# Sums of squares on VectorE only, the row factor one quarter later in the feed-forward, and the rotation tables made later

## The chip, the cores and the metric

The kernel runs on one core of a Trainium2 chip. Its time is the device time of one launch in microseconds (us). A time is the median of several runs; beside it stands one execution that was taken with the hardware profiler, from which all rows come. TensorE is called PE in the rows, its weight load PEld, VectorE DVE, ScalarE ACT, GpSimd POOL, and SyncE SP.

## The reference

One sequence of 512 tokens of width 1024 in float32 goes through a block of two layers and then a second block. Cut to what matters:

```
x = x + 0.5 * swiglu(rmsnorm(x, g), w_gate, w_up, w_down)   # first feed-forward of a layer
x = x + mixed(rmsnorm(x, g)) @ w_out                        # pooling and dilated attention with rotated q and k
x = x + 0.5 * swiglu(rmsnorm(x, g), ...)                    # second feed-forward of the layer
...                                                         # the second layer, a final rmsnorm
x = x + second_mix(rmsnorm(x, g)); x = x + swiglu(rmsnorm(x, g), ...); out = rmsnorm(x, g)

def rmsnorm(x, g):  return x * rsqrt(mean(x * x, axis=-1) + 1e-6) * g
def rope_tables(positions):  ang = positions * inv_freq;  return cos(ang), sin(ang)
```

So there are five feed-forwards and three mixes, each with a norm ahead of it, and a norm at the end.

## The kernel before, in words

x lies transposed in eight tiles `x[c]` of 128 x 512 (width on partitions, tokens along a row). All large products are made in three passes of a two-part float32: an operand is split into a high part (`yh`, `wh`, on ACT) and a low part (`yl` at L456, `wl` at L371, on DVE), and PE makes high x high, low x high and high x low (L407 to L409 and L627 to L629).

**The norm.** The products are made of the raw x times the gain. The factor per token, 1/sqrt(mean square), comes in afterwards. `square` (L458) adds the squares of the eight tiles into `ss`: the first is written by ACT (L461), each other is squared into `sq` by ACT (L467), or by DVE (L465) for four tiles at the start, and added at L468, by GpSimd (`eng=G`) or by VectorE (`V`, the last two tiles, or every fourth). `row_factor` (L483) sums `ss` over the partitions by matmuls with ones (`tst`, L487) and takes the inverse root on DVE in some dozen small steps (L489, L476 to L481, the result is `rf`). `spread` (L501) turns the factor by PE into a row for each partition (`tbc`, L498) that ACT copies to `rbc` (L505). The evacuations of the first products multiply by `rbc` (`cc`, L568).

**The feed-forward** (`ffn`, L540) goes through eleven pairs of 256 columns in four phases. The first pair is plain: the quarters T11, T12, T21 and T22 of 24 matmuls of 128 x 512 each. Every other pair is made of seven products (W11, S1, S2, W12, S3, S4, W22) of 24 matmuls of 128 x 256; S1, S2 and the like take sums of quarters of x as an operand (`r`, L437 to L440, split into `rh`, L442, and `rl`, L443) and sums of weights (`wt`). W11 of the second pair writes a bank (`x1`) that one of the plain pair's results lay in, so it follows that result's evacuation. Each turn of the loop gives out one product; `row_factor` is called after turn 0 (T11) and `spread` after turn 1.

**The start** (L1559 on) loads x, splits and squares it, makes the rotation tables (`rope_tables`, L704, some 28 small DVE instructions and two ACT sines), and goes into the first feed-forward.

The order on each engine isn't that of the code line by line: a scheduler orders the instructions of each engine at build time by its own estimate, and the engines then keep to that order. What an edit moves is read from the order of each engine.

The places of the program, in time: the start (first feed-forward of layer 0); from mix 0 to the second feed-forward; from there to the first feed-forward of layer 1; from mix 1 to the second feed-forward of layer 1; mix 2; from mix 2 to the last feed-forward; the end.

Of the kernel before, what the change touches and what calls it, by code (L numbers as in the profile page):

```python
# [28 lines left out]
D = 1024  # L29
KC = D // P  # L30
# [13 lines left out]
G_FFN1, G_MIX, G_FFN2, G_FIN, G_MIX2, G_FFN3, G_FIN2, G_AB, G_PROD = 0, 2, 4, 6, 7, 8, 9, 10, 11  # L44
# [62 lines left out]
D_ORDER = (0, 4, 1, 5, 2, 6, 3, 7)  # L107
# [115 lines left out]
def tile_blocks(tc, A, out):  # L223
    nc = tc.nc
    V, ACT, G, PE = nc.vector, nc.scalar, nc.gpsimd, nc.tensor

    with (
# [14 lines left out]
        def tbank(name="tp"):  # L242
            return pst.tile([P, S], F32, name=name, tag="tp")
# [3 lines left out]
        x = [keep.tile([P, S], F32, name=f"x{c}") for c in range(KC)]  # L247
# [11 lines left out]
        def gain(i, c):  # L259
            return gains[:, i * KC + c : i * KC + c + 1]  # L260
# [150 lines left out]
        def cut(hl, *ix):  # L411
            return hl[0][ix], hl[1][ix]
# [3 lines left out]
        sums = {}  # L416
# [9 lines left out]
            return pair[c]  # L426

        def square_x(c):
            square(x[c], c == 0, V if c >= KC - 2 else G)

        def sums_of(c, g):

            b1, b2 = (state["ffn"].tile([P, 2, HALF], F32, name="b", tag="snap", bufs=3) for _ in range(2))
            r = state["ffn"].tile([P, 4, HALF], F32, name="r", tag="wt", bufs=2)
            ACT.activation(b1, x[c], AF.Copy, scale=gain(g, c))
            ACT.activation(b2, x[c + 4], AF.Copy, scale=gain(g, c + 4))
            V.tensor_sub(r[:, 0], b1[:, 0], b1[:, 1])  # L437
            V.tensor_sub(r[:, 2], b2[:, 1], b1[:, 1])
            V.scalar_tensor_tensor(r[:, 1], b2[:, 1], -1.0, r[:, 0], op0=ALU.mult, op1=ALU.subtract)
            V.scalar_tensor_tensor(r[:, 3], r[:, 1], -1.0, b2[:, 0], op0=ALU.mult, op1=ALU.subtract)  # L440
            h, l = rest[c] = [state["ffn"].tile([P, 4, HALF], F32R, name=f"r{e}{c}", tag=f"r{e}{c}", bufs=1) for e in "hl"]
            ACT.activation(h, r, AF.Copy)  # L442
            V.tensor_sub(l, r, h.bitcast(F32))  # L443
# [11 lines left out]
            ACT.activation(h, src, AF.Copy, scale=g)  # L455
            V.scalar_tensor_tensor(l, src, g, h.bitcast(F32), op0=ALU.mult, op1=ALU.subtract)  # L456

        def square(src, first, eng=G, on_vector=False):  # L458
            if first:
                sums["s"] = small.tile([P, S], F32, name="ss", tag="ss", bufs=1)  # L460
                ACT.activation(sums["s"], src, AF.Square)  # L461
            else:
                sq = small.tile([P, S], F32, name="sq", tag="sq", bufs=2)
                if on_vector:
                    V.tensor_mul(sq, src, src)  # L465
                else:
                    ACT.activation(sq, src, AF.Square)  # L467
                eng.tensor_add(sums["s"], sums["s"], sq)  # L468

        def rsqrt(r, v):  # L470

            n = r.shape[1]
            it = small.tile([P, 8], I32, name="rsi", tag="rsi")
            t = small.tile([P, 8], F32, name="rst", tag="rst")
            it, t = it[:, :n], t[:, :n]
            V.tensor_scalar(it, v.bitcast(I32), 1, None, op0=ALU.logical_shift_right)  # L476
            V.tensor_scalar(r.bitcast(I32), it, -1, 0x5F3759DF, op0=ALU.mult, op1=ALU.add)
            for _ in range(3):
                V.tensor_mul(t, r, r)
                V.scalar_tensor_tensor(t, t, -0.5, v, op0=ALU.mult, op1=ALU.mult)  # L480
                V.scalar_tensor_tensor(r, t, 1.5, r, op0=ALU.add, op1=ALU.mult)  # L481

        def row_factor(s, n, name):  # L483

            o = tbank("tst")
            for i in range(TC):
                PE.matmul(o[:, i : i + 1], s[:, i * P : (i + 1) * P], ones, start=True, stop=True)  # L487
            v = small.tile([P, TC], F32, name="rv", tag="rv")
            V.tensor_scalar(v, o[:, :TC], 1.0 / n, EPS, op0=ALU.mult, op1=ALU.add)  # L489
            r = small.tile([P, TC], F32, name=name, tag="rfac", bufs=6)  # L490
            rsqrt(r, v)
            return r

        def spread_out(r):

            o = tbank("tbc")
            for i in range(TC):
                PE.transpose(o[:, i * P : (i + 1) * P], r[:, i : i + 1].to_broadcast([P, P]), ident)  # L498
            return o

        def spread(r, b=None):  # L501
            o = spread_out(r)
            if b is None:
                b = small.tile([P, S], F32, name="rbc", tag="rbc", bufs=1)
            ACT.copy(b, o)  # L505
            return b
# [30 lines left out]
                t, j = [p.rearrange("p a b -> p (a b)") for p in rest[c]], ("S1", "S2", "S3", "W22").index(name)  # L537
            return cut(t, slice(None), slice(j * HALF, (j + 1) * HALF))

        def ffn(coef, nxt, gain_of=None):  # L540
            pool = state["ffn"]
            a, got, cc, snap = {}, {}, {}, {}
            later = []
# [11 lines left out]
            def flat(t, half):  # L555
                return t[:, half].rearrange("p a b -> p (a b)")
# [37 lines left out]
            def evac(t, o):  # L594
                if len(t) == 2:
                    d = t[1]
                    V.scalar_tensor_tensor(x[d], o, coef, x[d], op0=ALU.mult, op1=ALU.add)  # L597
                    if t[0] == len(PHASES) - 1:
                        nxt(d)
                    return  # L600
                _, p, n = t
                if n == "W12":
                    V.tensor_add(flat(chunk(2 * p), 0), o[n], snap["W11"])
                elif n == "S3":
                    V.scalar_tensor_tensor(flat(chunk(2 * p + 1), 1), o[n], -1.0, snap["S1"], op0=ALU.mult, op1=ALU.subtract)
                elif n == "S4":
                    V.tensor_add(flat(chunk(2 * p), 1), o[n], snap["S2"])
                    finish(2 * p)
                elif n == "W22":
                    finish(2 * p + 1)  # L610
                elif n in ("T12", "T22"):
                    finish(n == "T22", o)
# [29 lines left out]
            for i, t in enumerate(ffn_plan()):  # L642
                w = take()
                if len(t) == 2:
                    ks = [f for p in PHASES[t[0]] for f in (2 * p, 2 * p + 1)]
                    while any(f not in a for f in ks):
                        rest_of()
                    od = tbank("dn")
                    for k, f in enumerate(ks):
                        mm3(od, cut(w, slice(None), slice(k * P, (k + 1) * P)), a[f], k == 0, k == len(ks) - 1)  # L650
                    now = t, od
                elif t[2] in PLAIN:
                    if i % 2 == 0:
                        o = [xbank(j, "mm") for j in range(2)]
                    plain(o, w, i // 2, i % 2)
                    now = t, o
                else:
                    n = t[2]
                    if n == "W11":
                        o = {}  # L660
                        o["W11"] = o["S2"] = o["S3"] = o["W22"] = xbank(0, "x1")
                    elif n == "S1":
                        o["S1"] = o["S4"] = xbank(1, "x3")
                    elif n == "W12":
                        o["W12"] = xbank(2, "x2")
                    product(o[n], w, n, n in ("W11", "S1", "W12"))
                    now = t, dict(o)
                if before:
                    evac_act(*before)
                highs(state["next"] + SPLIT)  # L670
                if before:
                    evac(*before)
                rest_of()
                lows(state["next"] + SPLIT)
                before = now
                if i == 0:
                    r = row_factor(sums["s"], D, "rf")
                if i == 1:
                    got["rb"] = spread(r)
                if i < 4 and gain_of is not None:  # L680
                    sums_of(i, gain_of)
            evac(*before)


# [861 lines left out]
            return f  # L1546

        def square_d(d):
            square(x[d], d == 0, V if d % 4 == 3 else G)

        def next_mix(g):
            def f(d):
                split(d, g)
                square_d(d)

            return f
# [6 lines left out]
        with layers():  # L1563
            for c in range(KC):
                split(c, G_FFN1)
                if c == 0:
                    ahead(1)
            ahead(2)
            for c in range(KC):
                square(x[c], c == 0, V if c >= KC - 2 else G, c % 2 == 1)  # L1570
            rope_tables()
            ffn(0.5, next_mix(G_MIX), G_FFN1)
        mix(0, G_FFN2)
        with layers(G_FFN2):
            ffn(0.5, next_ffn(G_FFN1 + 1), G_FFN2)
# [7 lines left out]
        rb = spread_out(row_factor(sums["s"], D, "rf"))  # L1583
# [22 lines left out]
```

## Time and profile before

| what | value |
|---|---|
| median of 3 runs | 2533.16 us (2532.66 to 2533.94) |
| profiled execution, its own time | 2529.62 us |
| its span (first to last instruction) | 2527.8 us |
| PE busy | 2462.2 us, 97% of the span |
| DVE busy | 1964.1 us, 78% |
| ACT busy | 1315.2 us, 52% |
| POOL busy | 343.9 us, 14% |

PE is the engine to look at: what isn't its work is a wait, a start or an end. A busy share hides where the waits are, and a PE that is busy at half its clock counts as busy too; so the rows further down are read by place. The profiled execution took 1.8 us more than its span, and 3.5 us less than the median.

### The profile page before, as it was taken

The numbers are of one execution on the slowest core, as the hardware profiler recorded it, in microseconds if no ns is written. First come the engines' busy times: TensorE is split into PE (matmuls) and PEld (weight loads), VectorE is DVE, ScalarE is ACT, GpSimd is POOL, SyncE is SP. The second block draws the span as 40 slices with busy tenths as digits, with TensorE's granted clock in tenths as the row PEclk, the third lists the DMA queues.
The fourth block names the chain that finished last, engine by engine and source line by source line (L and its number), as shares of the span: only waits on it lengthen the run. The fifth ranks groups of instructions, "written<-read, shape, count | busy, mean of one in ns | idle before, by whom it ended". The sixth has DMA issues, their size and how long they took to land.

```text
span 2527.8 us, 39773 instructions
## 1 busy us (share of the span) xinstructions
PE 2462.2 (97%) x15714; PEld 2217.4 (88%) x15714; DVE 1964.1 (78%) x2895; ACT 1315.2 (52%) x2065; POOL 343.9 (14%) x498
## 2 busy tenths in 40 slices
PE   7999999999999999999999999999999999999997
PEld 6999988887999988999988888999988887799996
DVE  8887764788887778877755889887767887988775
ACT  5444443676544455444444676444455775654442
POOL 1000014432000000000014431000013553100001
PEclk8999999999999999999999999999999999999999
DMA  4333232213233332333232113333233311323322
GB/s 160 109 100 104 74 100 88 57 40 105 88 117 100 103 107 80 102 109 103 80 93 86 43 42 113 111 101 105 73 101 95 98 42 41 118 92 105 105 65 77
DMA packets 73338, 229.72 MB, mean 91 GB/s; under 512 B 9536, under 2 KB 9920, under 8 KB 73152
## 3 DMA queue, kind: packets, MB, share of 16 engines
q1 hardware_dynamic: 73152, 227.19, 29.1%
q8 instruction: 123, 2.02, 0.3%
q14 instruction: 63, 0.52, 0.1%
HBM read 225.06 MB, written 2.10 MB: 90 GB/s over the span
## 4 chain that ended last, share of the span: by engine, by line
PE 84%; DVE 10%; ACT 3%; issue 2%; POOL 1%; DMA 1%; SPq 0%; DVEq 0%; ACTq 0%; POOLq 0%
PE x L629 13%; PE x L628 13%; PE x L627 13%; PE dn L407 8%; PE dn L408 8%; PE dn L409 8%; PE mm L407 5%; PE mm L408 5%; PE mm L409 4%; DVE wl L371 2%; PE ov L1028 2%; PE tp L1010 1%; PE mm L767 1%; PE mm L768 1%; DVE yl L456 1%
## 5 line engine op out<-in xcount | busy, mean ns | idle before, releaser
L627 PE MATMUL x<-rh,wh 128*128 128x256 f32 x1600 | 454.6, 284 | 4.0 <-ACT rh L442 3.8
L628 PE MATMUL x<-rl,wh 128*128 128x256 f32 x1600 | 454.6, 284 | 2.3 <-DVE rl L443 2.3
L629 PE MATMUL x<-rh,wl 128*128 128x256 f32 x1600 | 454.6, 284 | 0.0
L363 ACT ACTIVATE wh<-wd 128x768 fp32r<-128x768 f32 (+2 forms) x265 | 237.5, 896 | 348.6 <-PE x L628 173.6
L407 PE MATMUL dn<-ah,wh 128*128 128x512 f32 x880 | 344.0, 391 | 0.1
L408 PE MATMUL dn<-al,wh 128*128 128x512 f32 x880 | 343.8, 391 | 0.0
L409 PE MATMUL dn<-ah,wl 128*128 128x512 f32 x880 | 342.3, 389 | 0.0
L627 PE MATMUL x<-yh,wh 128*128 128x256 f32 x1200 | 339.7, 283 | 0.3 <-ACT wh L363 0.3
L628 PE MATMUL x<-yl,wh 128*128 128x256 f32 x1200 | 339.7, 283 | 0.0
L629 PE MATMUL x<-yh,wl 128*128 128x256 f32 x1200 | 339.6, 283 | 0.0
L627 PEld LDWEIGHTS x<-rh,wh 128*128 128x128 f32 x1600 | 308.5, 193 | 7.2 <-ACT rh L442 4.2
L363 ACT ACTIVATE wh<-wr 128x1024 fp32r<-128x1024 f32 (+1 forms) x178 | 187.5, 1054 | 241.6 <-PE x L628 88.9
L628 PEld LDWEIGHTS x<-rl,wh 128*128 128x128 f32 x1600 | 308.7, 193 | 5.0 <-DVE rl L443 2.7
L468 POOL TENSOR_TENSOR ss<-ss,sq 128x512 f32<-128x512 f32 x48 | 72.5, 1510 | 1762.3 <-ACT sq L467 1739.4
L629 PEld LDWEIGHTS x<-rh,wl 128*128 128x128 f32 x1600 | 308.4, 193 | 0.4 <-DVE wl L371 0.3
L371 DVE TENSOR_TENSOR wl<-wd,wh 128x768 fp32r<-128x768 f32 (+2 forms) x265 | 272.7, 1029 | 45.9 <-ACT wh L363 43.2
L371 DVE TENSOR_TENSOR wl<-wr,wh 128x1024 fp32r<-128x1024 f32 (+1 forms) x166 | 209.2, 1262 | 71.9 <-ACT wh L363 71.2
L627 PEld LDWEIGHTS x<-yh,wh 128*128 128x128 f32 x1200 | 230.2, 192 | 3.2 <-ACT wh L363 0.9
L628 PEld LDWEIGHTS x<-yl,wh 128*128 128x128 f32 x1200 | 230.3, 192 | 2.3
L629 PEld LDWEIGHTS x<-yh,wl 128*128 128x128 f32 x1200 | 230.1, 192 | 0.0
L597 DVE SCALAR_TENSOR_TENSOR x<-dn,x 128x512 f32<-128x512 f32 x160 | 110.0, 688 | 116.0 <-PE dn L409 116.0
L409 PEld LDWEIGHTS dn<-ah,wl 128*128 128x128 f32 x880 | 165.3, 188 | 35.3
(331 smaller groups left out, 5433.2 us busy)
## 6 DMA issues: line engine op xcount, KB each, us to landing
wr<-in_w SPq DMA_DIRECT2D x175, 512.0 KB, 3.6
wd<-in_w SPq DMA_DIRECT2D x120, 384.0 KB, 3.1
wq<-in_w SPq DMA_DIRECT2D x78, 512.0 KB, 3.6
wd<-in_w SPq DMA_DIRECT2D x55, 512.0 KB, 3.7
wd<-in_w SPq DMA_DIRECT2D x40, 256.0 KB, 3.1
x<-in_xT SPq DMA_DIRECT2D x8, 256.0 KB, 6.3
out<-x SPq DMA_DIRECT2D x8, 256.0 KB, 2.0
bias<-in_consts SPq DMA_DIRECT2D x2, 448.0 KB, 4.1
```

The costliest lines, as they stand in the source:

```text
L363: ACT.activation(h[:, :n], src[:, :n], AF.Copy)
L371: state["low"] = eng.tensor_sub(l[:, :n], src[:, :n], h[:, :n].bitcast(F32)).ins
L407: PE.matmul(o, w[0], xx[0], start=start, stop=False)
L408: PE.matmul(o, w[0], xx[1], start=False, stop=False)
L409: PE.matmul(o, w[1], xx[0], start=False, stop=stop)
L456: V.scalar_tensor_tensor(l, src, g, h.bitcast(F32), op0=ALU.mult, op1=ALU.subtract)
L468: eng.tensor_add(sums["s"], sums["s"], sq)
L597: V.scalar_tensor_tensor(x[d], o, coef, x[d], op0=ALU.mult, op1=ALU.add)
L627: PE.matmul(oo, wh, xh, start=start and j == 0 and c == 0, stop=False, skip_group_check=True)
L628: PE.matmul(oo, wh, xl, start=False, stop=False, skip_group_check=True)
L629: PE.matmul(oo, wl, xh, start=False, stop=c == 3, skip_group_check=True)
L1028: PE.matmul(o, w, part, start=(j == 0 and n == 0), stop=(j == TC - 1 and n == 1))
```

## The change

Three edits:

1. Every addition into `ss` (L468) is made on VectorE; the 48 that GpSimd made move there, 18 were there already. At the start the four squares that DVE made (L465) are made by ACT.
2. In `ffn`, `row_factor` is called in turn 1 and `spread` in turn 2, each ahead of that turn's evacuations, in place of the ends of turns 0 and 1.
3. `rope_tables` isn't called ahead of the first feed-forward, but handed to it as `aside`, and called behind the first down product of the third phase.

```
         def square_x(c):
-            square(x[c], c == 0, V if c >= KC - 2 else G)
+            square(x[c], c == 0)
...
-        def square(src, first, eng=G, on_vector=False):
+        def square(src, first, on_vector=False):
...
-                eng.tensor_add(sums["s"], sums["s"], sq)
+                V.tensor_add(sums["s"], sums["s"], sq)
...
-        def ffn(coef, nxt, gain_of=None):
+        def ffn(coef, nxt, gain_of=None, aside=None):
...
+                if i == 1:
+                    r = row_factor(sums["s"], D, "rf")
+                if i == 2:
+                    got["rb"] = spread(r)
                 if before:
                     evac_act(*before)
...
-                if i == 0:
-                    r = row_factor(sums["s"], D, "rf")
-                if i == 1:
-                    got["rb"] = spread(r)
                 if i < 4 and gain_of is not None:
                     sums_of(i, gain_of)
+                if aside and t == (2, D_ORDER[0]):
+                    aside()
...
-            square(x[d], d == 0, V if d % 4 == 3 else G)
+            square(x[d], d == 0)
...
-                square(x[c], c == 0, V if c >= KC - 2 else G, c % 2 == 1)
-            rope_tables()
-            ffn(0.5, next_mix(G_MIX), G_FFN1)
+                square(x[c], c == 0)
+            ffn(0.5, next_mix(G_MIX), G_FFN1, rope_tables)
```

The order on PE at the start, before: `tst` stands among the last products of the second 24-matmul quarter, `tbc` ten matmuls ahead of the first L627, which is W11 of the second pair.

```order
L407 MATMUL mm<-yh_138,wh 128x512
L408 MATMUL mm<-yl_139,wh 128x512
L409 MATMUL mm<-yh_138,wl 128x512
L487 MATMUL tst<-ones,ss 128x1 x4
L407 MATMUL mm<-yh_142,wh 128x512
...
L498 MATMUL tbc<-consts,rf 128x128 x4
L409 MATMUL mm<-yh_130,wl 128x512
...
L409 MATMUL mm<-yh_142,wl 128x512
L627 MATMUL x_429<-yh_108,wh 128x256
```

The same place on PE with the change.

```order
L407 MATMUL mm<-yh_122,wh 128x512
L408 MATMUL mm<-yl_123,wh 128x512
L487 MATMUL tst<-ones,ss 128x1 x4
L409 MATMUL mm<-yh_122,wl 128x512
...
L407 MATMUL mm<-yh_142,wh 128x512
L408 MATMUL mm<-yl_143,wh 128x512
L409 MATMUL mm<-yh_142,wl 128x512
L498 MATMUL tbc<-consts,rf 128x128 x4
L627 MATMUL x_389<-yh_108,wh 128x256
```

`tst` moved by 11 matmuls, into the third quarter, and `tbc` to the place directly ahead of W11. In the other feed-forwards the same two moved as well. From mix 0 to its feed-forward `tst` comes 24 matmuls later, and of the 29 matmuls between `tbc` and W11 10 are left; from the second feed-forward to the first of layer 1 24 of 38 are left, and from mix 2 to the last feed-forward 12 of 23.

The order on DVE from mix 0 to its feed-forward, before: `x_78` to `x_81` are the last four tiles of x, `yl_6239` to `yl_6251` their low parts, and five additions into `ss` are on POOL.

```order
L443 TENSOR_TENSOR rl_6319<-r,rh_6318 128x1024
L468 TENSOR_TENSOR ss<-ss,sq 128x512
L972 TENSOR_TENSOR x_81<-mm,x_81 128x512
L456 SCALAR_TENSOR_TENSOR yl_6239<-x_78,gains,yh_6238 128x512
L456 SCALAR_TENSOR_TENSOR yl_6243<-x_79,gains,yh_6242 128x512
L468 TENSOR_TENSOR ss<-ss,sq 128x512
L456 SCALAR_TENSOR_TENSOR yl_6247<-x_80,gains,yh_6246 128x512
L456 SCALAR_TENSOR_TENSOR yl_6251<-x_81,gains,yh_6250 128x512
L371 TENSOR_TENSOR wl<-wr,wh 128x1024
```

The same place on DVE with the change (its lines have moved by two, L974 is L972 of before).

```order
L438 TENSOR_TENSOR r<-b 128x256
L468 TENSOR_TENSOR ss<-ss,sq 128x512
L974 TENSOR_TENSOR x_80<-mm,x_80 128x512
L439 SCALAR_TENSOR_TENSOR r<-b,r 128x256
L456 SCALAR_TENSOR_TENSOR yl_6239<-x_78,gains,yh_6238 128x512
L456 SCALAR_TENSOR_TENSOR yl_6243<-x_79,gains,yh_6242 128x512
L468 TENSOR_TENSOR ss<-ss,sq 128x512
L974 TENSOR_TENSOR x_81<-mm,x_81 128x512
L456 SCALAR_TENSOR_TENSOR yl_6247<-x_80,gains,yh_6246 128x512
L371 TENSOR_TENSOR wl<-wr,wh 128x1024
L468 TENSOR_TENSOR ss<-ss,sq 128x512
L456 SCALAR_TENSOR_TENSOR yl_6251<-x_81,gains,yh_6250 128x512
```

All seven additions are in DVE's row now, and `rl_6319` with the steps that lead to it stands behind the last `yl`.

The order on DVE at the rotation tables with the change; before, they begin with the cast of `pi`, right behind the last addition into `ss`, and lie between the steps of `row_factor`.

```order
L605 SCALAR_TENSOR_TENSOR cc<-x_389,snap 128x512
L712 CAST pf<-pi 128x4
L371 TENSOR_TENSOR wl<-wr,wh 128x1024
L714 TENSOR_TENSOR ang<-pf,consts 128x32
L727 TENSOR_SCALAR n<-ang 128x32
L728 TENSOR_SCALAR n<-n 128x32
```

They begin some fifty rows later than before, behind the first results of the second pair (`x_389` is W11's bank), and not where the call stands in the code.

## Rows read from the trace of the kernel before

**Rows 1.** The page, first part: engines, busy us (share) and count.

```profile
PE 2462.2 (97%) x15714; PEld 2217.4 (88%) x15714; DVE 1964.1 (78%) x2895; ACT 1315.2 (52%) x2065; POOL 343.9 (14%) x498
```

**Rows 2.** Waits of PE: us in total, times, longest us.

```profile
PE tst L487 <- DVE ss L468: 6.0, 4, 2.2
PE mm L408 <- DVE yl L456: 4.8, 5, 2.5
...
PE tst L487 <- POOL ss L468: 0.4, 1, 0.4
```

**Rows 3.** One line of the code, L468: count, ns minimum/median/maximum.

```profile
L468 POOL TENSOR_TENSOR ss<-ss,sq x48: 1279/1362/2324, 7.9 to 2505.9; 128x512 f32<-128x512 f32 x48
...
L468 DVE TENSOR_TENSOR ss<-ss,sq x18: 676/685/693, 21.8 to 2513.9; 128x512 f32<-128x512 f32 x18
```

**Rows 4.** Timeline of PE at the start: start, length, [idle before <-releaser].

```profile
25.03 1.44 PE L487 MATMUL tst<-ones,ss 128*128 128x1 f32 x8 [2.75 <-DVE pf L710]
...
48.37 0.39 PE L628 MATMUL x<-rl,wh 128*128 128x256 f32 x1 [0.88 <-DVE rl L443]
```

**Rows 5.** Windows: length, busy us of PE, PEld, DVE, ACT, POOL, then PE's granted clock.

```profile
25.47:32.30 6.83, 6.83 (x20) 5.57 (x20) 5.80 (x21) 4.37 (x6) 0.00 (x0) 0.50 0.58 187
57.00:100.00 43.00, 43.00 (x328) 41.53 (x327) 37.20 (x42) 21.85 (x29) 0.00 (x0) 1.00 0.35 109
600.00:640.00 40.00, 37.81 (x194) 31.80 (x193) 38.53 (x62) 25.63 (x35) 5.03 (x3) 1.00 0.30 95
628.24:634.59 6.35, 6.35 (x29) 5.25 (x28) 6.28 (x9) 5.10 (x6) 0.00 (x0) 1.00 0.15 28
```

**Rows 6.** Timeline of DVE at the start.

```profile
14.58 4.80 DVE L456 SCALAR_TENSOR_TENSOR yl<-x,gains,yh 128x512 fp32r<-128x512 f32 x4
...
21.85 0.69 DVE L468 TENSOR_TENSOR ss<-ss,sq 128x512 f32<-128x512 f32 x1 [1.19 <-POOL ss L468]
...
27.79 0.17 DVE L726 TENSOR_SCALAR n<-n 128x32 f32<-128x32 f32 x1
27.88 0.16 DVE L476 TENSOR_SCALAR rsi<-rv 128x4 int32<-128x4 int32 x1
...
39.77 0.69 DVE L568 TENSOR_TENSOR cc<-mm,rbc 128x512 f32<-128x512 f32 x1 [1.22 <-ACT rbc L505]
```

**Rows 7.** Timeline of DVE from mix 0 to its feed-forward.

```profile
595.76 0.74 DVE L456 SCALAR_TENSOR_TENSOR yl<-x,gains,yh 128x512 fp32r<-128x512 f32 x1
...
597.03 1.19 DVE L456 SCALAR_TENSOR_TENSOR yl<-x,gains,yh 128x512 fp32r<-128x512 f32 x1
...
601.32 1.77 DVE L456 SCALAR_TENSOR_TENSOR yl<-x,gains,yh 128x512 fp32r<-128x512 f32 x1
...
607.80 1.51 DVE L439 SCALAR_TENSOR_TENSOR r<-b,r 128x256 f32<-128x256 f32 x1
...
609.56 0.41 DVE L440 SCALAR_TENSOR_TENSOR r<-r,b 128x256 f32<-128x256 f32 x1
```

**Rows 8.** Timeline of POOL at the same place.

```profile
600.22 2.32 POOL L468 TENSOR_TENSOR ss<-ss,sq 128x512 f32<-128x512 f32 x1 [0.51 <-ACT sq L467]
```

**Rows 9.** Timeline of PE at the same place.

```profile
615.68 1.05 PE L487 MATMUL tst<-ones,ss 128*128 128x1 f32 x8 [1.32 <-DVE ss L468]
...
627.50 0.65 PE L498 MATMUL tbc<-consts,rf 128*128 128x128 f32 x4 [0.87 <-DVE rf L481]
```

**Rows 10.** Timeline of PE, second feed-forward to the first of layer 1.

```profile
960.51 0.50 PE L408 MATMUL mm<-yl,wh 128*128 128x512 f32 x1 [1.00 <-DVE yl L456]
965.11 1.05 PE L487 MATMUL tst<-ones,ss 128*128 128x1 f32 x8 [1.14 <-DVE ss L468]
```

**Rows 11.** Timeline of DVE at the same place.

```profile
939.60 2.08 DVE L371 TENSOR_TENSOR wl<-wd,wh 128x768 fp32r<-128x768 f32 x1
...
942.53 0.94 DVE L371 TENSOR_TENSOR wl<-wd,wh 128x768 fp32r<-128x768 f32 x1
```

**Rows 12.** Timeline of PE from mix 2 to the last feed-forward.

```profile
2166.64 0.50 PE L408 MATMUL mm<-yl,wh 128*128 128x512 f32 x1 [2.47 <-DVE yl L456]
```

## The prediction

> **What bounds the kernel now.** I read the engines first [rows 1]: PE is busy 97% of the span, so with its work unchanged only its idle time, its clock and its start can give anything; DVE at 78% isn't the bound on the whole, but a mean over stages says nothing of the places where PE waits. So I read the waits of PE next [rows 2]: the reader is to see that `tst` and the products that take `yl` wait for DVE, and that what they wait for is the sums of squares or what stands behind them in DVE's row. Then I read the timelines at those places, and the windows for how full DVE is there: 38.5 of 40 us from 600 to 640 [rows 5]. There the kernel is bound by DVE, just around the norms, and there the change adds work to DVE. That is the question of this case.
>
> **What an addition costs on either engine.** GpSimd takes 1.36 us at the median, DVE 0.69 [rows 3]; instructions of DVE overlap at the ends (0.17 long, 0.09 to the next [rows 6]), so I count 0.61. On the face of it 48 additions are 29 us more for DVE, less 2.4 for the four squares that go to ACT. But the additions on POOL aren't free for DVE. A `yl` alone takes 0.74; at 597.03 and 601.32 it takes 1.19 and 1.77, and at 607.80 a step of `r` 1.51 where it takes 0.41 alone [rows 7]. Each of them lies beside an addition of POOL: that of 600.22 runs until 602.54 [rows 8], and the `yl` that began at 601.32 ends 0.55 behind it, as if it had waited for it and only then begun. Five DVE instructions are lengthened so from 597.03 to 607.80, one for each of the five additions of POOL there, by 0.45, 1.03 and 1.10 us in the rows shown; five at their mean of 0.86 are 4.3 us, and as the first of them is the least I take 3.7, against 5 x 0.61 = 3.05 to be paid. So an addition costs DVE slightly less when DVE makes it itself. That holds where the neighbours read two tiles in SBUF, which is so wherever `yl`, `wl`, `r` and x are made.
>
> The Trainium skill (SBUF — State Buffer, "Who interferes with whom") gives a rule for this: a VectorE instruction with two SBUF inputs and a GpSimd instruction that reads SBUF contend for one pair of ports, and the second to start is held until the first is done. The trace agrees in the 0.55 us above. By the rule alone an addition on POOL gives back anything from nothing (POOL starts second) to its whole 1.36 us, five of them 0 to 6.8, where the rows give 3.7.
>
> Another page speaks against the change: the Trainium skill (Perfetto Trace Analysis, "Optimizing Scalar/DVE Operations") says that from a saturated VectorE work may be moved to ScalarE or even GpSimd, and adds that between VectorE and GpSimd this might not help. The first half would have this change lose time around 600 us (the first rival below), the second half is what the lengthened rows bear out.
>
> **The start.** Before, `tst` waits 2.75 us [rows 4]. The view names the cast `pf`, which `tst` doesn't read; it stands directly behind the last addition, and that is what `tst` needs. Behind this wait PE runs at half its clock for 6.83 us [rows 5], which is 3.4 us of loss, say 2.9 as not all there is matmul columns. Now the five additions of POOL are gone: the four `yl` from 14.58 take 4.80 [rows 6] where alone they would take 4 x 0.67 = 2.7. All waits for `yl` are 4.8 [rows 2]; less 1.00 and 2.47 of other places [rows 10, 12] 1.3 is left for the start, which goes as well. `tst` comes 11 matmuls later, 2.5 us at 0.23 (29 matmuls, two of them cut, in 6.35 us [rows 5]), and the sums come 2.6 us earlier (DVE loses 2.1 us of lengthening, 2.4 of squares and 1.2 of waiting for POOL, and gets 3.05 of additions). Together 5 us, more than the wait: so it shouldn't wait, and the clock shouldn't fall there. Against it stands a new wait: `tbc` now lies directly ahead of W11, whose bank is free only after `rbc` and an evacuation, and behind W11 all of PE is queued. DVE waited 1.22 us for `rbc` and took 0.69 for the `cc` [rows 6]; less the end of `tbc` I give it 1.3. PE's account until W11: 2.75 + 2.9 + 1.3 - 1.3 = 5.7, and 0.4 for `tst` itself, which ran at the low clock: 6.1. Next PE stands at S1, where it waits for `rl` [rows 4], so DVE's account decides from there: 2.1 + 2.4 - 3.05 + 28 small instructions of the rotation tables at 0.09 = 2.5, and the idle time that DVE spent on POOL's addition, 1.19 [rows 6]: 5.1, and up to 2.3 more if its other idle time, of the size of the 1.22 ahead of `cc`, shrinks with PE's wait. Between 5.1 and 7.4 by the one and at 6.1 by the other, which leaves 0.5 of the low clock out, I take **7.0**, as DVE's idle time there is what the wait for `tst` made; the ends are 4 (S1 takes back what W11 gained) and 9 (no wait at W11).
>
> The rotation tables lie now between 50 and 85 us. From 57 to 100 DVE is busy 37.2 of 43 us and PE has no gap [rows 5]: 5.8 us of cover for 2.5 us. I give them nothing; with the cover gone they cost 2.5. The DMA of the positions moves behind some weight loads in SP's queue; only the cast waits for it, and that stands tens of us later.
>
> **Mix 0 and mix 1 to their feed-forwards.** `tst` waits 1.32 and `tbc` 0.87 [rows 9]; around 1549 the same pattern stands. The last `yl` are made about 2 us earlier (0.6 net of the additions, and the `rl` with the steps of `r` that now stand behind them, over 1.2 us), `tst` comes 24 matmuls or 5.5 us later: its wait goes. `tbc` comes 38 matmuls behind `tst` in place of 43, 1.1 us less for the same chain of small steps on a full DVE, so of its 0.87 some may stay or come back: 0 to 0.8 of new wait. W11, ten matmuls or 2.3 us behind `tbc`, is just covered (1.22 + 0.69 = 1.9). Gain **1.9** each, from 0.5 to 2.2.
>
> **Second feed-forward to the first of layer 1.** The waits are 1.00 and 1.14 [rows 10]. Here each addition of POOL holds up a `wl` or a step of `r`: 2.08 in place of 0.94 [rows 11]. At 1.0 for each of five, 5 us against 3.05 paid: x and `yl` come 2 us earlier, and both waits go. Gain **2.1**, from 1.0 to 2.2.
>
> **Mix 2.** A `tst` waits 0.4 for POOL [rows 2]; gain **0.4**, from 0 to 0.7.
>
> **Mix 2 to the last feed-forward.** The wait of 2.47 for `yl` [rows 12]: DVE comes out only about 0.4 earlier, but four matmuls of the next quarter are drawn ahead into it (0.9) and `tst` leaves the place. Later S1 waits for `rl`, as at the start, so DVE decides how much of it is kept. 0.4 + 0.9 is the least likely to be lost, and `tst` (1.05 long in rows like [rows 9]) gives some more: gain **1.6**, from 0.5 to 2.5.
>
> **Elsewhere.** From feed-forward to mix PE has no gap, DVE has room, the change gives nothing and costs nothing; without that room each such place would cost up to 3 us. At the end the last additions were DVE's before, and the chain behind them is unchanged: nothing.
>
> **Sum.** 7.0 + 1.9 + 1.9 + 2.1 + 0.4 + 1.6 = 14.9 us. The profiled execution, 2529.62 with its span of 2527.8 and 1.8 around it, comes to 2514.7; the median shown is 3.5 above it, so I take the sum from the median: 2533.16 - 14.9 = **2518.3 us**.
>
> **The rivals.**
> 1. DVE becomes the bound (slower). If the lengthening isn't given back, for instance since it falls where DVE would have waited anyway, each of the seven stretches from x to a norm gets 3.05 us more of DVE work. At the four places where DVE is full that goes to PE: from a refund of under 0.61 an addition on it loses. With nothing given back and no gain but that of the start it is 4 x 3.05 - 7.0 = 5.2 us slower, 2538; with half of 3.7 given back 4 x 1.2 - 7.0, 2 us faster. For it speaks 38.5 of 40 us [rows 5]; against it the lengthened rows [rows 7, 11]. Chance 0.05.
> 2. W11 waits in every feed-forward. If `rf` is late, `tbc`, `rbc` and `cc` come in front of W11 and cost 1 to 1.5 us at four places: 14.9 - 5 = 10 us gained, 2523. For it: the chain from `tst` to `tbc` is shorter by some matmuls and late already [rows 9]. Chance 0.2.
> 3. The start gives back: W11 comes earlier but S1 waits for `rl` until nearly its old time, or the clock falls elsewhere (3.4 us, as it fell once [rows 5]). Start 2 to 4 in place of 7: 2521 to 2523. Chance 0.15.
> 4. No change that can be measured (within 0.2%, 5.1 us, which is about what a measurement tells apart): gains of the start returned and the rest taken by rival 2, 2528 to 2533. Or the change doesn't do what it says: the additions weren't what `tst` waited for. Chance 0.08.
> The forecast, 2514 to 2521, has 0.5; the last 0.02 is for more than forecast, by a clock that falls nowhere: 2510.
>
> **Range and chances.** 2510 to 2528 takes in the forecast and rivals 2 and 3. Faster by over 0.2% (under 2528.1) 0.87, within 0.08, slower 0.05.
>
> **What would show it.** Right: no GpSimd row of L468, `yl` near 0.74 at all places, `tst` without a wait at the start and at full clock, a wait of about 1.3 ahead of W11 there, the `rl` wait of S1 ending near 41 in place of 48.4, no `tst` wait at the two mixes. Wrong: a `yl` or `wl` wait of PE of over 2 us around 600, 955 or 1540; W11 waiting at all places; the half clock at 25 us still there; `yl` of 1.2 us or more with POOL idle beside them, which would take away the reading of the lengthened rows.

## The result and the profile after

The changed kernel takes 2514.36 us (median of 6 runs, 2513.11 to 2518.21), the one before 2532.2 in the same comparison (6 runs): the ratio is 0.9937, with a 95% interval of 0.9926 to 0.9948, so 16 us faster (13 to 19; the two medians lie 17.8 apart). The forecast was 2518.3, with 2510 to 2528 as its range. The profiled execution has a span of 2511.2 us, 16.6 less than before.

The page of after, first part.

```profile
PE 2456.4 (98%) x15714; PEld 2217.5 (88%) x15714; DVE 1970.4 (78%) x2939; ACT 1317.3 (52%) x2069; POOL 274.5 (11%) x450
```

DVE has 44 instructions more and is busy only 6.3 us longer, where 48 additions less four squares at 0.61 are 26.9: over the program 20.6 us were given back by other rows, 0.43 for each addition that left POOL. They came back at five places alone. Added up over the rows of before that stand beside an addition of POOL, against the same rows in after, the lengthening was 4.1 us at the start, 3.7 at mix 0, 5.2 ahead of layer 1, 3.7 at mix 1 and 3.3 behind mix 2, 20.0 in all for 25 additions. At the places of the other 23 DVE's rows are lengthened by as much after as before. Two of the five lengthened rows at mix 0 aren't in [rows 7]; with them the five are 0.45, 0.44, 1.03, 0.66 and 1.09 us too long:

```profile
599.08 1.18 DVE L456 SCALAR_TENSOR_TENSOR yl<-x,gains,yh 128x512 fp32r<-128x512 f32 x1
605.06 1.08 DVE L438 TENSOR_TENSOR r<-b 128x256 f32<-128x256 f32 x1 [1.37 <-ACT b L436]
```

The waits of PE in after: us, times, longest.

```profile
PE x L628 <- DVE rl L443: 2.7, 2, 1.8
PE tbc L498 <- DVE rf L481: 2.4, 1, 2.4
PE x L627 <- ACT rh L442: 2.3, 1, 2.3
PE tst L487 <- DVE ss L468: 2.2, 1, 2.2
...
PE tp L1465 <- DVE ptl L1287: 1.5, 1, 1.5
PE x L627 <- DVE cc L568: 1.4, 1, 1.4
...
PE mm L408 <- DVE yl L456: 0.9, 1, 0.9
```

Against [rows 2]: the waits of `tst` for `ss` and of `tbc` for `rf` that are left are those of the last norm, and one wait for `yl` is left of five. New are the wait for `cc` and that of `tp` (L1465), inside mix 2.

The start, timeline of PE in after.

```profile
22.45 1.02 PE L487 MATMUL tst<-ones,ss 128*128 128x1 f32 x8
...
34.52 0.38 PE L627 MATMUL x<-yh,wh 128*128 128x256 f32 x1 [1.40 <-DVE cc L568]
...
40.80 0.39 PE L628 MATMUL x<-rl,wh 128*128 128x256 f32 x1 [1.80 <-DVE rl L443]
```

`tst` waits for nothing, W11 waits 1.40 for the evacuation, and the wait for `rl` ends 7.6 us earlier than in [rows 4]. The windows of after, in the columns of [rows 5].

```profile
22.45:29.28 6.83, 6.83 (x35) 5.81 (x35) 6.81 (x22) 3.90 (x7) 0.00 (x0) 1.00 0.44 171
42.30:49.10 6.80, 5.94 (x25) 5.05 (x24) 6.80 (x8) 3.43 (x4) 0.00 (x0) 0.50 0.36 89
600.00:640.00 40.00, 40.00 (x250) 35.94 (x249) 38.20 (x62) 24.42 (x31) 0.00 (x0) 1.00 0.22 66
57.00:100.00 43.00, 43.00 (x321) 41.19 (x320) 41.35 (x69) 22.82 (x33) 0.00 (x0) 1.00 0.31 94
```

The clock stays at its upper level (2.4 GHz) behind `tst`; a fall to the lower one (1.2 GHz) behind the wait for `rl` is still there (42.3, in before 49.4). From 600 to 640 PE has no gap although DVE is as full as before. The rotation tables are covered: PE is busy in all 43 us from 57 on.

DVE in after, at the start and from mix 0 to its feed-forward.

```profile
13.28 2.73 DVE L456 SCALAR_TENSOR_TENSOR yl<-x,gains,yh 128x512 fp32r<-128x512 f32 x4
```
```profile
586.89 0.74 DVE L456 SCALAR_TENSOR_TENSOR yl<-x,gains,yh 128x512 fp32r<-128x512 f32 x1
587.55 0.68 DVE L468 TENSOR_TENSOR ss<-ss,sq 128x512 f32<-128x512 f32 x1
588.15 0.74 DVE L456 SCALAR_TENSOR_TENSOR yl<-x,gains,yh 128x512 fp32r<-128x512 f32 x1
```

The four `yl` take 2.73 us in place of 4.80 [rows 6], and no `yl` there is longer than 0.74 where it was up to 1.77 [rows 7].

Where the 16.6 us came from is read off the starts of one and the same instruction in both traces (first down product, W11 of each feed-forward, `tst` of mix 2, and one L409 matmul inside mix 0 and one inside mix 1):

| stretch | before to after, at its end | gained | forecast |
|---|---|---|---|
| start, to the first down product | 74.16 to 66.81 | 7.3 | 7.0 |
| until inside mix 0 | 472.50 to 463.66 | 1.5 | 0 |
| to W11 after mix 0 | 634.60 to 623.17 | 2.6 | 1.9 |
| to W11 of layer 1 | 983.22 to 968.11 | 3.7 | 2.1 |
| until inside mix 1 | 1404.32 to 1390.44 | -1.2 | 0 |
| to W11 after mix 1 | 1567.67 to 1551.38 | 2.4 | 1.9 |
| to `tst` of mix 2 | 2142.11 to 2127.40 | -1.6 | 0.4 |
| to the last feed-forward's first down product | 2216.43 to 2199.81 | 1.9 | 1.6 |

A second profile of each kernel (the first runs of the next section) says how far these lines can be trusted. Those from inside mix 0 to W11 (2.6) and from inside mix 1 to W11 (2.5 there) come out again, the 3.7 of layer 1 as 5.3, with a fall of the clock at 963.3 in that profile of before. The 1.5 until inside mix 0 doesn't: the second profile of before needs 396.8 us for that stretch, as the changed kernel does, and the first 398.3, with the clock at its lower level for 3.4 us from 469.2. The -1.2 until inside mix 1 comes again: behind a wait of 1.7 us for `prob` that both kernels have, the clock falls in both profiles of the changed kernel and in neither of before. Of all traces here those with one of the first two edits have this fall and the three without don't. But behind the same wait in mix 0 it fell in one profile of before and not in the other, so the wait alone doesn't decide it; whether the change does, no run tells.

The -1.6 inside mix 2 (-0.9 between the second profiles) has a cause of the change's own. POOL, after:

```profile
2056.23 2.38 POOL L371 TENSOR_TENSOR wl<-wr,wh 128x1024 fp32r<-128x1024 f32 x1
```

DVE, after:

```profile
2056.71 2.17 DVE L1106 SCALAR_TENSOR_TENSOR u<-gq,gh 128x256 f32<-128x256 f32 x1
```

The same step on DVE, before:

```profile
2073.08 0.41 DVE L1104 SCALAR_TENSOR_TENSOR u<-gq,gh 128x256 f32<-128x256 f32 x1
```

POOL still makes some of the `wl`. With the changed order one of them begins 0.48 us ahead of `u` and not behind it; `u` takes 2.17 us in place of 0.41 and ends 0.27 behind POOL, and PE's `tp` (L1465) waits 1.46 for the `ptl` that stands behind it. All ten traces of kernels with the additions on VectorE have this wait, none of the four others; the clock falls behind it at 2059.6 in both profiles of the changed kernel.

### The profile page after: what moved, and what is told of

The parts are those of the page before. It is cut to its first block, busy times and chain, and to the rows that moved or that the text cites. A ratio compares the mean times of both kernels' runs of the same rounds, so it can differ in the third digit from the quotient of the medians.

```text
span 2511.2 us, 39735 instructions
## 1 busy us (share of the span) xinstructions
PE 2456.4 (98%) x15714; PEld 2217.5 (88%) x15714; DVE 1970.4 (78%) x2939; ACT 1317.3 (52%) x2069; POOL 274.5 (11%) x450
## 4 chain that ended last, share of the span: by engine, by line
PE 88%; DVE 7%; ACT 2%; issue 1%; POOL 1%; DMA 0%; DVEq 0%; SPq 0%; ACTq 0%; POOLq 0%
PE x L629 13%; PE x L628 13%; PE x L627 13%; PE dn L407 8%; PE dn L408 8%; PE dn L409 8%; PE mm L407 6%; PE mm L408 6%; PE mm L409 6%; PE ov L1030 2%; PE tp L1012 2%; DVE wl L371 1%; PE mm L769 1%; PE mm L770 1%; PE ov L1307 1%
## 5 line engine op out<-in xcount | busy, mean ns | idle before, releaser
L627 PE MATMUL x<-rh,wh 128*128 128x256 f32 x1600 | 454.4, 284 | 3.0 <-ACT rh L442 2.3
L409 PE MATMUL dn<-ah,wl 128*128 128x512 f32 x880 | 342.3, 389 | 0.0
L627 PE MATMUL x<-yh,wh 128*128 128x256 f32 x1200 | 339.8, 283 | 1.7 <-DVE cc L568 1.4
L627 PEld LDWEIGHTS x<-rh,wh 128*128 128x128 f32 x1600 | 308.5, 193 | 5.9 <-ACT rh L442 2.5
L627 PEld LDWEIGHTS x<-yh,wh 128*128 128x128 f32 x1200 | 230.2, 192 | 5.0 <-DVE cc L568 1.8
L409 PEld LDWEIGHTS dn<-ah,wl 128*128 128x128 f32 x880 | 165.2, 188 | 35.3
L407 PEld LDWEIGHTS dn<-ah,wh 128*128 128x128 f32 x880 | 165.7, 188 | 31.3
L408 PEld LDWEIGHTS dn<-al,wh 128*128 128x128 f32 x880 | 165.7, 188 | 29.8
```

The lines of the kernel that those rows point to most:

```text
L407: PE.matmul(o, w[0], xx[0], start=start, stop=False)
L408: PE.matmul(o, w[0], xx[1], start=False, stop=False)
L409: PE.matmul(o, w[1], xx[0], start=False, stop=stop)
L627: PE.matmul(oo, wh, xh, start=start and j == 0 and c == 0, stop=False, skip_group_check=True)
```

## The experiments

Ratios are to the kernel before, with the 95% interval; 0.001 is 2.5 us.

**The kernel before and the changed one, again.**

> The kernel before, once more: how far one and the same kernel differs from itself in this comparison, and whether its waits at the start stand in a second profile as in the first. Both theories: ratio 1.000 within its interval, tst waiting 2 to 3 us at the start, the half clock behind it.

> The changed kernel once more, on the chip of the next three: 0.9937 of the kernel before as measured first, within 0.001; at the start W11 waits 1.4 us for cc and S1 1.8 us for rl, and the clock halves behind that.

Measured 0.9999 (0.9990 to 1.0008) and 0.9936 (0.9923 to 0.9948). At the start both repeat their waits to 0.01 us, `tst` 2.74 in the one, W11 1.40 and S1 1.81 in the other. But the first down product of the kernel before starts at 72.67, 1.5 earlier than in its first profile: behind S1 the clock was low for 3.4 us there, for 6.8 in the first profile.

**One edit at a time.** Each of the first three is the kernel before with the lines of one edit of the diff; the last two have two of the edits.

> Only the sums of squares are added on VectorE (and the start's four squares made on ScalarE); row factor and rotation tables stay as before. Theory A (an addition on GpSimd holds up VectorE about as long as the addition costs VectorE itself, and keeps tst waiting): most of the gain is here, 10 to 13 us of some 16: the start without the 2.75 us wait of tst and without the half clock behind it (about 5), about 3.5 from the second feed-forward to layer 1, 1 to 1.5 at each of mix 0 and mix 1. Theory B (VectorE is full there, so 27 us more work on it brings nothing by itself, and only the later row factor takes waits away): the start alone gains, 5 at most, and the wait of PE for yl around 600, 955 and 1545 grows; 5 us faster at most, or slower.

Measured 0.9953 (0.9940 to 0.9967), 12 us faster. Theory A holds. The timeline of PE at the start, and from mix 0 to its feed-forward:

```profile
21.90 0.95 PE L487 MATMUL tst<-ones,ss 128*128 128x1 f32 x8
...
34.36 0.38 PE L627 MATMUL x<-yh,wh 128*128 128x256 f32 x1 [0.92 <-DVE cc L568]
```
```profile
607.61 0.95 PE L487 MATMUL tst<-ones,ss 128*128 128x1 f32 x8
...
617.63 0.60 PE L498 MATMUL tbc<-consts,rf 128*128 128x128 f32 x4
```

No `tst` and no `tbc` waits, though after mix 0 `row_factor` stands in its old turn. At the start the scheduler moved `tst` by seven of the 11 matmuls in this kernel too (by all 11 where the tables are later as well, below), so that move doesn't come from the edit of `row_factor`.

> Only the row factor is taken one quarter later; additions and rotation tables stay as before. Theory A: the waits of tst go at mix 0, mix 1 and before layer 1 (1.3 to 1.5 us each), those for yl and for the sums at the start stay: 3 to 5 us faster. Theory B: this edit has nearly the whole gain, over 10 us.

Measured 0.9984 (0.9975 to 0.9992), 4 us faster, as theory A says, but not as it divides it. The timeline of PE:

```profile
24.93 1.02 PE L487 MATMUL tst<-ones,ss 128*128 128x1 f32 x8 [0.92 <-DVE pf L710]
...
39.36 0.36 PE L627 MATMUL x<-yh,wh 128*128 128x256 f32 x1 [1.90 <-DVE n L727]
```
```profile
615.78 0.95 PE L487 MATMUL tst<-ones,ss 128*128 128x1 f32 x8
...
625.00 0.65 PE L498 MATMUL tbc<-consts,rf 128*128 128x128 f32 x4 [1.99 <-DVE rf L481]
```

After mix 0 the 1.32 of `tst` [rows 9] goes, and `tbc` waits 1.99 in place of 0.87: between mix 0's `tbc` (419.88 to 415.65) and W11 (634.60 to 630.30) the gain is 0.1 us. A wait only changed its name. What this edit gains alone are 1.7 us ahead of layer 1 and up to 4.2 at the start (1.5 of it may be one execution's clock), where `tst` waits 0.92 in place of 2.75 and the clock doesn't fall.

> Only the rotation tables are made later. Theory A: VectorE has 28 small instructions less at the start, 2.5 us, but tst still waits for GpSimd's additions there: 0 to 2.5 us faster. Theory B (the tables, between the steps of the row factor, made it late): over 4 us faster.

Measured 1.0006 (0.9996 to 1.0016): no gain that can be measured, the lower end of what theory A allowed. `tst` still waits 2.38 us at the start.

> Additions on VectorE and the tables later, the row factor's place as before. Theory A: the start as with the whole change (7 us), 2.5 to 3.5 before layer 1, at mix 0 and mix 1 tst waits again for the last addition, so 0.5 to 1.5 there: 12 to 14 us faster. Theory B: 7 us at most.

Measured 0.9950 (0.9937 to 0.9962), 12.6 us faster. Its W11 after mix 0 starts at 622.75 and that of layer 1 at 968.06, where the whole change has 623.17 and 968.11. The waits of `tst` at the two mixes, which theory A expected back, didn't come. So up to layer 1 the later row factor adds nothing to the additions. From `tst` of mix 2 to the first down product 0.4 us are gained here and 1.9 in the changed kernel. That isn't shown to be the row factor's: here the clock falls for 6.8 us in that stretch, in the changed kernel for 3.4, and in the kernel with writes beside, further down, which has the later row factor too, it falls for 6.8 and 0.4 is gained. By the intervals this kernel isn't to be told from the whole change.

> The changed kernel with the rotation tables made ahead of the first feed-forward again. Theory A (28 small instructions are in VectorE's way at the start): W11 or S1 of the start comes 1 to 2.5 us later, the rest as in the changed kernel: 1 to 2.5 us slower than it. Rival (they lie in gaps of VectorE there too): the same.

Measured 0.9945 (0.9931 to 0.9959), not to be told from the whole change. Its first down product starts at 68.20, 1.4 us later than in the changed kernel; its W11 waits longer at the start:

```profile
36.23 0.39 PE L627 MATMUL x<-yh,wh 128*128 128x256 f32 x1 [2.53 <-DVE cc L568]
```

So in this profile the tables cost 1.4 us where they stood, once `tst` doesn't hide them; as the clock was low for 3.4 us there and for 6.8 in the changed kernel, the size is uncertain.

**Is it GpSimd's reading that held up VectorE?** Two kernels have PE, DVE and ACT in the order of the changed one, row by row, and more work on POOL, whose results nobody reads.

```
 V.tensor_add(sums["s"], sums["s"], sq)
+if beside:                       # where GpSimd added before
+    G.tensor_add(z, src, src)
```

> The changed kernel with 45 more additions on GpSimd (x tile + x tile into a tile that nobody reads), at the places where GpSimd added into ss before; the order on PE, DVE and ACT is that of the changed kernel, row by row. Theory A (GpSimd's additions hold up VectorE's two-input instructions): yl, wl and r are lengthened as before, to 1.2 to 2.1 us, the waits of PE for yl and rl come back at the start, at mix 0, mix 1, before layer 1 and before the last feed-forward: 4 to 10 us slower than the changed kernel, 2519 to 2525. Theory B (the gain came only from tst no longer standing behind GpSimd's slow chain, lengthened rows are a chance of the timeline): within 1.5 us of the changed kernel.

Measured 0.9981 (0.9972 to 0.9990): 2524.98 us at the median, 11 us slower than the changed kernel by the ratios (0.0044). Theory A holds, at the upper end and a little over it, though not all waits are where it put them: `tst` waits 0.94 at the start, `tbc` 1.60 and 1.65 at the two mixes, the products with `yl` 0.92 ahead of layer 1 and 1.73 behind mix 2. DVE and POOL of this kernel at mix 0:

```profile
588.85 1.23 DVE L371 TENSOR_TENSOR wl<-wr,wh 128x1024 fp32r<-128x1024 f32 x1
589.99 1.53 DVE L456 SCALAR_TENSOR_TENSOR yl<-x,gains,yh 128x512 fp32r<-128x512 f32 x1
...
595.58 1.52 DVE L470 TENSOR_TENSOR ss<-ss,sq 128x512 f32<-128x512 f32 x1
```
```profile
588.90 2.07 POOL L474 TENSOR_TENSOR dz<-x 128x512 f32<-128x512 f32 x1 [13.63 <-DVE x L980]
```

The order of starts decides who waits: POOL's addition began 0.05 us behind `wl` and took 2.07 (1.04 at the least in this kernel), and the `yl` behind that ends at 591.52, 0.55 after POOL's 590.97. Its page:

```profile
PE 2459.2 (98%) x15714; PEld 2216.9 (88%) x15714; DVE 1999.0 (79%) x2939; ACT 1317.3 (52%) x2069; POOL 340.4 (13%) x495
```

DVE is busy 28.6 us longer than in the changed kernel with the same instructions: 0.64 us for each of the 45 additions beside it, as much as an addition of its own (0.61).

This kernel is still 5 us faster than the kernel before (0.0019). There GpSimd's additions also stood in the chain ahead of `tst`, at 1.36 us each; here they don't, and at the start 0.94 us of the wait of 2.75 are back. So the hold on VectorE is shown to cost time, but how the 16 us divide between it and the slower chain isn't: the additions here begin at other times than those of before, and no run has the slow chain without the hold.

```
+    G.tensor_copy(z[:, :1], src[:, :1])
+    G.memset(z, 0.0)             # three times
```

> The same places, but GpSimd copies one column of x and then writes the spare tile with a constant three times, so that it is busy about as long and hardly reads. Theory A in its narrow form (only a GpSimd instruction that reads holds up VectorE's two-input instructions): within 1.5 us of the changed kernel, yl at 0.75. In its wide form (any GpSimd instruction beside it holds VectorE up): 4 to 10 us slower, as with the additions.

Measured 0.9942 (0.9929 to 0.9955): the narrow form holds. DVE and POOL of it:

```profile
587.07 0.75 DVE L456 SCALAR_TENSOR_TENSOR yl<-x,gains,yh 128x512 fp32r<-128x512 f32 x1
587.74 0.69 DVE L470 TENSOR_TENSOR ss<-ss,sq 128x512 f32<-128x512 f32 x1
588.34 0.75 DVE L456 SCALAR_TENSOR_TENSOR yl<-x,gains,yh 128x512 fp32r<-128x512 f32 x1
```
```profile
587.25 0.53 POOL L475 MEMSET dz<- 128x512 f32 x1
587.84 0.53 POOL L476 MEMSET dz<- 128x512 f32 x1
588.42 0.53 POOL L477 MEMSET dz<- 128x512 f32 x1
```

POOL works right beside DVE and nothing is lengthened, though POOL as a whole is busy longer (378.9 us) than with the additions (340.4): it isn't that POOL is busy, but that it reads. That is the rule of the Trainium skill (SBUF — State Buffer, "Who interferes with whom"), which names only GpSimd instructions that read SBUF for this case, and the trace agrees: VectorE is busy 28.6 us longer with the reads and 1.2 less (1969.2) with the writes.

**What is left of the start.** The changed kernel with `sums_of`, which makes the operands of S1, called earlier; in the second the row factor is also back in its old turns, for the first feed-forward alone; in the third `sums_of` is earlier wherever it is called.

```
-if i < 4 and gain_of is not None:
-    sums_of(i, gain_of)
+if i < 4 and gain_of is not None:
+    for c in range(4)[2 * i : 2 * i + 2] if aside else (i,):   # third: without the condition
+        sums_of(c, gain_of)
```

> The changed kernel, with the operands of S1 at the start (sums_of) made two a turn in the first two turns, so that the last rl stands six rows earlier on VectorE. Theory A (what is left of the start is VectorE's order: S1 waits for the last rl, and the clock falls behind that wait): the 1.8 us of S1 go, W11 still waits 1.4 us, the half clock goes if no wait stands near it: 1.5 to 5 us faster than the changed kernel. Rival (VectorE is full there, so that the wait only moves from rl to the next weights wl of S1 or S2): within 1 us of it.

> As the run before, and at the start the row factor back in its old turns, which puts tbc ten matmuls ahead of W11 again. Theory A: W11 doesn't wait (tbc to rbc to cc is 1.9 us, ten matmuls are 2.3), nor S1 for rl: 3 to 6 us faster than the changed kernel. Rival (the start is bound by VectorE's work as a whole): the waits move to wl of S1 or S2, within 1.5 us of it.

> The operands of S1 two a turn in all three feed-forwards that make them there, not at the start alone. At mix 0, mix 1 and mix 2 the order then puts tbc one or two matmuls ahead of W11. Theory A (W11 waits for tbc, rbc and cc where fewer than about nine matmuls stand between): W11 waits 1 to 1.5 us at mix 0 and mix 1, at mix 2 S1's wait of 2.3 and 0.9 us shrinks instead: 0 to 3 us slower than the run with the start alone. Rival (cc isn't late there): no wait of W11, 0 to 3 us faster than it.

Measured 0.9922 (0.9909 to 0.9934), 0.9919 (0.9906 to 0.9933) and 0.9936 (0.9924 to 0.9949), where the changed kernel had 0.9936 beside them. In the first nothing waits for `rl`, but W11 waits 2.34 in place of 1.40, and the clock falls for 3.4 us behind that. The second is 4 us faster than the changed kernel, 2510.65 us at the median, though the intervals of the two overlap a little and it isn't to be told from the first. In the trace its first down product starts at 62.12 against 66.81. Its start, timeline of PE:

```profile
30.39 0.60 PE L498 MATMUL tbc<-consts,rf 128*128 128x128 f32 x4
...
37.24 0.38 PE L627 MATMUL x<-rh,wh 128*128 128x256 f32 x1 [0.85 <-ACT wh L363]
...
39.02 0.39 PE L629 MATMUL x<-rh,wl 128*128 128x256 f32 x1 [1.28 <-DVE wl L371]
```

Neither W11 nor `rl` is waited for, as theory A says; the wait has in part moved to weights, as the rival says, but 2.1 us are left of 3.9 (1.40, 1.80 and 0.67 for weights in the changed kernel), and the clock doesn't fall there. Windows of the changed kernel, of this one, and of the kernel with writes beside, which has the order and the waits of the changed one:

```profile
24.00:60.00 36.00, 31.93 (x203) 28.96 (x202) 33.22 (x59) 17.85 (x22) 0.00 (x0) 0.91 0.24 71
```
```profile
24.00:60.00 36.00, 33.87 (x242) 31.44 (x241) 35.68 (x53) 20.05 (x27) 0.00 (x0) 1.00 0.23 70
```
```profile
24.00:60.00 36.00, 31.13 (x213) 28.33 (x213) 34.68 (x62) 18.01 (x23) 0.31 (x1) 1.00 0.25 81
```

In the third window the clock stays up behind the same waits (1.40 and 1.81), and from W11 to the first down product that kernel needs 1.6 us less than the changed one. So some 1.6 of the 4.7 us between 62.12 and 66.81 are the clock of single executions, not the order. With DVE busy 35.68 of 36 us there is next to no gap left on it at the start.

In the third kernel `tbc` came to stand one or two matmuls ahead of W11 behind all mixes, and W11 waits there, with a fall of the clock behind it; timeline and window of PE:

```profile
621.15 0.60 PE L498 MATMUL tbc<-consts,rf 128*128 128x128 f32 x4
...
623.82 0.38 PE L627 MATMUL x<-yh,wh 128*128 128x256 f32 x1 [1.84 <-DVE cc L568]
```
```profile
624.90:628.30 3.40, 3.40 (x19) 3.40 (x18) 3.00 (x5) 0.63 (x1) 0.00 (x0) 0.50 0.00 0
```

That is theory A of its expectation, and the second rival of the prediction, at more than its price of 1 to 1.5: 1.84 of wait and half of 3.4 at the low clock are 3.5 us, which is what this kernel loses at mix 1 against the first of the three. Behind mix 2 it gains 2.6, as S1's waits go. In all it takes back what the start gives: 3.5 us slower than the first by the ratios, a little more than theory A allowed.

## Why the prediction was right, step by step

**What an addition costs on either engine** was the step on which all rested, and it held where DVE is full: additions on POOL lengthen DVE's rows with two inputs in SBUF (28.6 us by 45 of them, none by as much writing). At the two mixes 3.7 us came back, as taken, for 3.05 paid, and 5.2 ahead of layer 1, where I took 5. That the 3.7 was right to a tenth has some luck in it, since it was estimated from three of the five rows. Over the program the refund is smaller than the price, 0.43 for 0.61, and DVE's own work grew by 6.3 us, since elsewhere nothing came back; there DVE has room. Two details were wrong. The rows that make x aren't held: `x<-mm,x`, with one input in PSUM, takes 0.68 beside POOL at 596.43 and 598.47. And nine stretches have five such additions on POOL each, not seven; the first rival's sum uses four of them and doesn't change. That rival needed a refund near nothing at those places, which the lengthened rows rule out.

**The start**: 7.0 forecast, 7.3 measured, 5.9 against the second profile of the kernel before. `tst` without a wait, no fall of the clock, 1.3 of new wait at W11 (1.40), `rl` near 41 (40.80): all as said. The terms were less exact than their sum: two `yl` ahead of 14.58 were lengthened too (4.1 in all, where I counted 2.1), and GpSimd's chain ahead of `tst`, in the account only as 1.2 us of waiting, may be a larger part of the cause, as the kernel with additions beside has it. That the move of `tst` comes from the additions and the tables the prediction didn't ask.

**Mix 0 and mix 1 to their feed-forwards**: 1.9 each forecast, 2.6 and 2.4 measured. The cause was wrong in one half: "`tst` comes 24 matmuls or 5.5 us later: its wait goes". With the later `tst` alone the wait goes to `tbc`, and with the additions alone both go without a later place. What ends last there is DVE's row up to `rf`, not the place of `tst`. The size was short since I read the idle time in the rows as the loss. A row's idle time counts from the modelled end of a matmul, 0.39 long, while the next one usually starts 0.23 behind:

```profile
963.58 0.39 PE L409 MATMUL mm<-yh,wl 128*128 128x512 f32 x1
```

The `tst` that follows at 965.11 [rows 10] is 1.53 behind it; 1.30 is lost, not 1.14.

**Second feed-forward to the first of layer 1**: 2.1 forecast, 3.7 measured, the term most off. The mechanism is as said, both waits are gone; the same reading of idle time hid part (two waits, and three short delays from 952 on, 0.3, 0.2 and 0.2); from start to start all of it comes to 3.6.

**Mix 2**: 0.4 forecast, -1.6 measured. This step failed: I looked only at `tst` and not at what the new order does to the `wl` that POOL keeps. One of them now begins ahead of DVE's `u` and makes a new wait of 1.46, with a fall of the clock behind it.

**Until inside mix 0 and mix 1** nothing was forecast; 1.5 and -1.2 were measured. Both are falls of the clock, which I left out: the first comes and goes between two profiles of the kernel before, the second is in both profiles of the changed kernel and in neither of before.

**Mix 2 to the last feed-forward**: 1.6 forecast, 1.9 measured. The wait of 2.47 for `yl` shrank to 0.93, but the agreement is partly luck: with the same order and a longer fall of the clock only 0.4 is gained. That the later row factor does the work here isn't shown.

So the sum, 14.9 against 16.6 in the profiles, is better than its parts: the mixes and layer 1 were taken too small by 2.8, mix 2 too large by 2.0.

**The rivals.** The second happened at the start alone, with its price (1.40), and in the third kernel above at the mixes too. The third didn't: S1 kept what W11 gained. The additions alone give 12 of the 16 us and the later row factor alone 4. What the row factor and the tables add to the additions isn't clear of noise: 0.9953 with the additions alone, 0.9950 and 0.9945 with one of the other edits, 0.9937 with both.

## What to carry to other kernels

Here work that was moved to GpSimd for the sake of a full VectorE wasn't off VectorE, as both read SBUF: look for rows of instructions with two SBUF inputs that are longer beside it than alone, and price the move by those at the places where VectorE is full. Where it had room (23 of the 48 additions) nothing came back; leaving those on GpSimd wasn't tried. Look also at what GpSimd keeps: its rows move against VectorE's too, as in mix 2. When a wait is taken away by a move, look at who waits next on the same chain: here `tst` gave its wait to `tbc` until DVE's row itself got shorter. Read the loss of a wait from start to start of the instructions around it, not from the idle time alone.

## What the hardware showed that I had not expected

The order of starts shifted the price between the engines: POOL's 128x512 addition of x to itself, 1.04 us at its shortest, took 2.07 when `wl` had begun 0.05 us before it.

And the length of a wait didn't decide whether the clock fell. Behind 1.84 us at W11 after mix 0 it fell to the lower level (1.2 GHz) for 3.4 us; behind 1.99 of `tbc` at nearly the same place, with the later row factor alone, it stayed up; behind the wait of 1.7 inside mix 0 it fell in one profile of the kernel before and not in the other. So a gain read from one profile can be off by 1.6 us for each such fall.
